# Block products issued across the borders of their groups, with the sums chained in one PSUM bank

## The chip, the cores and the metric

One core of one Trainium2 chip runs the kernel. The metric is the device time of one execution, in microseconds, of which the median over runs is compared. The engines are named as in the profile: PE (TensorE matmuls), PEld (its weight loads), DVE (VectorE), ACT (ScalarE), POOL (GpSimd) and SP, whose queue issues the DMAs.

## What is computed

A decoder layer on 1024 tokens of width 1024 in float32. Three mixers (gated linear attention, mLSTM, forgetting attention) read one wide input projection; their outputs go through one projection each, are merged by sigmoid gates and projected out; a gated MLP with a causal convolution over time follows.

```python
h = rmsnorm(x, norm_mix)
proj = h @ w_in                                   # 1024 x 12312
y = [gla(...), mlstm(...), fox(...)]              # on pieces of proj
branch = jnp.einsum('btnw,nwd->btnd', jnp.stack(y, 2), w_branch)
x = x + jnp.sum(branch * sigmoid(gates + b_gate), 2) @ w_out
h = rmsnorm(x, norm_ffn)
u = causal_dwconv(h @ w_up, conv_w, conv_b)       # 1024 x 5632, three taps
a, g = jnp.split(u, 2, axis=-1)
x = x + (silu(g) * a) @ w_down                    # 2816 rows of w_down
return rmsnorm(x, norm_final)
```

## The kernel before

The four large products (w_in, w_branch, w_up, w_down) are done by a Strassen scheme with seven block products in place of eight. A **job** takes two 128-column units of weights, cut into four blocks a11, a12, a21, a22, and a right side that has been cut and combined into seven operands, `xc[1]` to `xc[7]`. Every float32 operand is split into a high and a low part (`split`, lines 105 to 107: a CAST on ACT, a subtraction on DVE), and a block product (`prod`, line 1081) is twelve matmuls of 128x128 by 128x512: high by high, high by low, low by high, for each of four k-tiles (nine for the first part of w_down, with three k-tiles).

`strassen` (line 1091) issues a job: the products 1 (a11), 5 (sum1), 2 (a12), 6 (sum2), 7 (sum3), 3 (sum4), 4 (a22), in this order. The four weight sums are made on POOL (`comb`, line 1105). Four PSUM banks named `pg` serve a job: a11 and a12 add up in the bank `ba`, sum1 and sum4 in `bc`, sum3 and a22 in `bd`, sum2 has `bb`. Between the two products of a bank its content has to be copied out, since it is a term of other outputs too:

```python
self.prod(ba, self.wsplit(a11, "a11"), xc[1], True)
s1 = keep(ba, "s1")                      # ACT copy, line 1110
...
self.prod(ba, self.wsplit(a12, "a12"), xc[2], False)
...
nc.vector.tensor_tensor(out=s1, in0=s1, in1=bb, op=ALU.add)          # line 1130
...
nc.gpsimd.tensor_tensor(out=s7, in0=s5, in1=s7, op=ALU.add)          # line 1144
```

The four results go to `post`, which adds two terms on DVE and stores (`to_dram`), keeps (`to_tiles`), multiplies by a gate (`merge_pair`, line 1035) or adds to the rows of the result (`down_pair`, line 1262; there POOL takes the terms that lie in SBUF, except in the last part).

The stages follow each other: 48 jobs of w_in, between which the three mixers are issued step by step; three branches of four jobs with w_branch, **the merge**; the output projection; 22 jobs of w_up with convolution and gate (`ffn_up`, line 1232); and w_down in three parts of 6, 8 and 8 k-tiles, four jobs each. Each merge branch and each part of w_down has a right side of its own. `combos` (line 994) makes its seven operands from DRAM: per operand four loads into tiles `yb`, up to four subtractions (tiles `T`, `yb`), four CASTs on ACT and four subtractions on DVE, whose outputs the profile names `x`. The operands lie in 28 fixed slots (`MAP_IN`, `MAP_FF`, `MAP_DN`, lines 36 to 38), so that a new one can be written only when the last job of the group before has used the old one. A list of due times (`due`, with LAG and LAGD) sets when a step of `combos` is issued. I call the stretch where the right side changes **a border**; there are six: gate jobs to branch 1, branch 1 to 2, 2 to 3, up to part 1 of down, part 1 to 2, 2 to 3.

Each engine works through its own queue in order. What stands in the queues is set by a scheduler that orders the instructions of the code by its own estimate of times.

## Time and profile before

| | |
|---|---|
| device time, median of 3 runs | 2527.85 us (2523.35 to 2533.06) |
| the profiled execution: span from first to last instruction | 2538.0 us; no other time of that execution is listed |
| PE busy | 2363.6 us, 93% of the span |
| DVE busy | 1954.1 us, 77% |
| ACT busy | 1255.0 us, 49% |
| POOL busy | 1110.9 us, 44% |
| mean granted TensorE clock | 0.970 of full speed |

The span of the profiled execution is already longer than the median of the runs, by 10.15 us or 0.4%. In the profile a line of `kernel.py` is mostly that of a helper (L99 is every matmul, L107 every low part), so that groups are told apart by the names of their tiles. Matmuls overlap: the duration of one (about 0.4 us) is longer than the distance from one to the next.

### The profile page before, as it was taken

The numbers are of one execution on the slowest core, as the hardware profiler recorded it, in microseconds if no ns is written. First come the engines' busy times: TensorE is split into PE (matmuls) and PEld (weight loads), VectorE is DVE, ScalarE is ACT, GpSimd is POOL, SyncE is SP. The second block draws the span as 40 slices with busy tenths as digits, with TensorE's granted clock in tenths as the row PEclk, the third lists the DMA queues.
The fourth block names the chain that finished last, engine by engine and source line by source line (L and its number), as shares of the span: only waits on it lengthen the run. The fifth ranks groups of instructions, "written<-read, shape, count | busy, mean of one in ns | idle before, by whom it ended". The sixth has DMA issues, their size and how long they took to land. (4 is left out here: it accounts for less than half of the span.)

```text
span 2538.0 us, 34484 instructions
## 1 busy us (share of the span) xinstructions
PE 2363.6 (93%) x11531; PEld 1948.1 (77%) x11531; DVE 1954.1 (77%) x3244; ACT 1255.0 (49%) x2521; POOL 1110.9 (44%) x1018
## 2 busy tenths in 40 slices
PE   6999999899999999999999889799889999978888
PEld 5888788777888888888878768689677777766666
DVE  7886577667777867777777989875888888887896
ACT  5344455455666645555555443344444444453353
POOL 5322265444545543323322347530554444457563
PEclk9999999999999999999999999899899999989899
DMA  3455354554444443433333654444132222235432
GB/s 127 139 165 183 98 171 156 161 160 146 157 138 143 135 149 127 130 122 121 127 127 125 216 172 151 138 138 162 63 116 84 83 75 75 75 115 191 125 112 92
DMA packets 186034, 335.60 MB, mean 132 GB/s; under 512 B 17352, under 2 KB 79336, under 8 KB 185344
## 3 DMA queue, kind: packets, MB, share of 16 engines
q1 hardware_dynamic: 185856, 333.40, 40.4%
q8 instruction: 91, 1.49, 0.2%
q14 instruction: 87, 0.71, 0.1%
HBM read 237.75 MB, written 95.58 MB: 131 GB/s over the span
## 5 line engine op out<-in xcount | busy, mean ns | idle before, releaser
L99 PE MATMUL pg<-x,a12h 128*128 128x512 f32 x744 | 248.3, 416 | 49.1 <-ACT s L1110 47.6
L99 PE MATMUL pg<-x,a22h 128*128 128x512 f32 x744 | 244.0, 408 | 19.2 <-ACT s L1110 13.7
L99 PE MATMUL pg<-x,sum2h 128*128 128x512 f32 x744 | 239.0, 400 | 15.8 <-DVE x L107 12.0
L99 PE MATMUL pg<-x,a11h 128*128 128x512 f32 x744 | 234.6, 396 | 4.8 <-DVE s L1130 2.9
L99 PE MATMUL pg<-x,sum1h 128*128 128x512 f32 x744 | 236.0, 397 | 2.7 <-ACT sum1h L106 2.0
L99 PE MATMUL pg<-x,sum3h 128*128 128x512 f32 x744 | 237.9, 400 | 0.6 <-DVE x L107 0.6
L99 PE MATMUL pg<-x,sum4h 128*128 128x512 f32 x744 | 233.6, 394 | 0.0
L99 PEld LDWEIGHTS pg<-x,a12h 128*128 128x128 f32 x744 | 143.0, 199 | 88.9 <-ACT s L1110 59.1
L99 PEld LDWEIGHTS pg<-x,a22h 128*128 128x128 f32 x744 | 142.9, 196 | 55.8 <-ACT s L1110 17.8
L99 PEld LDWEIGHTS pg<-x,sum2h 128*128 128x128 f32 x744 | 140.1, 191 | 51.3 <-DVE x L107 16.8
L1144 POOL TENSOR_TENSOR s<-s,s 128x512 f32<-128x512 f32 x94 | 132.2, 1406 | 100.5 <-ACT s L1110 87.6
L1110 ACT COPY s<-pg 128x512 f32<-128x512 f32 x280 | 162.1, 579 | 13.8 <-PE pg L99 13.7
L99 PEld LDWEIGHTS pg<-x,a11h 128*128 128x128 f32 x744 | 139.7, 190 | 35.4 <-issue 4.0
L99 PEld LDWEIGHTS pg<-x,sum1h 128*128 128x128 f32 x744 | 139.9, 191 | 31.6 <-ACT sum1h L106 2.4
L99 PEld LDWEIGHTS pg<-x,sum3h 128*128 128x128 f32 x744 | 140.2, 192 | 30.1 <-DVE x L107 1.3
L99 PEld LDWEIGHTS pg<-x,sum4h 128*128 128x128 f32 x744 | 139.9, 190 | 29.9 <-DVE x L107 0.8
L99 PE MATMUL pg<-x,a22l 128*128 128x512 f32 x372 | 151.8, 408 | 10.6 <-DVE a22l L107 10.6
L99 PE MATMUL pg<-x,sum3l 128*128 128x512 f32 x372 | 148.6, 399 | 6.7 <-DVE sum3l L107 6.7
L99 PE MATMUL pg<-x,sum4l 128*128 128x512 f32 x372 | 146.6, 394 | 6.3 <-DVE sum4l L107 6.3
L99 PE MATMUL pg<-x,a12l 128*128 128x512 f32 x372 | 151.5, 407 | 0.0
L99 PE MATMUL pg<-x,a11l 128*128 128x512 f32 x372 | 146.6, 394 | 1.0 <-DVE a11l L107 1.0
L99 PE MATMUL pg<-x,sum2l 128*128 128x512 f32 x372 | 146.7, 394 | 0.0
(472 smaller groups left out, 6585.2 us busy)
## 6 DMA issues: line engine op xcount, KB each, us to landing
up_raw<-in_w_up SPq DMA_DIRECT2D x46, 512.0 KB, 3.6
yb<-y_d SPq DMA_DIRECT2D x84, 256.0 KB, 3.0
yb<-in_w_dn SPq DMA_DIRECT2D x77, 256.0 KB, 3.1
gate_raw<-in_w_in SPq DMA_DIRECT2D x24, 512.0 KB, 3.7
g_d<-st SPq DMA_DIRECT2D x48, 256.0 KB, 2.4
br_raw<-in_w_br SPq DMA_DIRECT2D x24, 512.0 KB, 3.7
gth<-g_d SPq DMA_DIRECT2D x48, 256.0 KB, 2.6
f_d<-c SPq DMA_DIRECT2D x22, 512.0 KB, 2.6
```

Source lines behind the costliest of these rows:

```text
L99: self.nc.tensor.matmul(out, lhsT=lhsT, rhs=rhs, start=start, stop=stop, skip_group_check=skip)
L1110: nc.scalar.copy(out=t, in_=bank)
L1144: nc.gpsimd.tensor_tensor(out=s7, in0=s5, in1=s7, op=ALU.add)
```

## The change

All jobs of the first part (w_in and merge) become one list, all jobs of w_up and w_down another. A generator `products` gives the order of the block products over the whole list: the products 3 and 4 of a job are issued behind the first ones of the next. `gemms` issues the weight split of a product two products ahead of its matmuls. The sums are chained in one bank, `x`: products 1, 6, 7 and 4 of a job add up there, and the bank is read after each of the four; 5 and 3 share the bank `z`, 2 has `y` alone. So s1 + bb and s5 + s7 are no longer added by DVE and POOL. In the merge, up and down, `z` and `y` lie in the other four banks (`pa`). In down every partial sum is added to the result on DVE straight from PSUM, and nothing is copied. The steps of `combos` hang on the products of the last job of the group before. The convolution of a job of w_up is issued in steps between the products of the next ones.

```diff
-MAP_IN = {1: 0, 5: 4, 2: 8, 6: 12, 7: 16, 3: 20, 4: 24}
+MAP_IN = {1: 0, 5: 4, 6: 8, 2: 12, 7: 16, 3: 20, 4: 24}
...
+def products(jobs, lead=0):
...
+        yield j, 1
+        yield j, 5
+        if prev is not None:
+            yield prev, 3
+        yield j, 6
+        if prev is not None:
+            yield prev, 4
+        yield j, 2
+        yield j, 7
+        prev = j
+    yield prev, 3
+    yield prev, 4
...
-            t = pool.tile([P, 512], F32, tag="yb", name="yb", bufs=5)
+            t = pool.tile([P, 512], F32, tag="yb", name="yb", bufs=4)
...
-        hi = self.swp.tile([P, 512], F32R, tag="sh", name=f"{nm}h", bufs=5)
-        lo = self.swp.tile([P, 512], F32R, tag="sl", name=f"{nm}l", bufs=5)
+        hi = self.swp.tile([P, 512], F32R, tag="sh", name=f"{nm}h", bufs=4)
+        lo = self.swp.tile([P, 512], F32R, tag="sl", name=f"{nm}l", bufs=4)
...
+    def compute(self, job, p):
...
+        b = {1: "x", 6: "x", 7: "x", 4: "x", 5: "z", 3: "z", 2: "y"}[p]
+        b = getattr(job, b)
+        self.prod(b, job.w.pop(p), x, p in (1, 5, 2))
+        if acc is not None:
+            if p == 1 or p == 2:
+                acc(0, 0, b)
+            elif p == 6 or p == 3:
+                acc(0, 1, b)
+            elif p == 7:
+                acc(1, 1, job.z)
+                acc(1, 1, b)
+            elif p == 4:
+                acc(1, 0, b)
+        elif p == 1:
+            job.s1 = keep(b, "s1")
+        elif p == 5:
+            job.s5 = keep(b, "s5")
+        elif p == 6:
+            job.u2 = keep(b, "u2")
+        elif p == 2:
+            post(0, 0, job.s1, b)
+        elif p == 3:
+            post(0, 1, job.u2, b)
+        elif p == 7:
+            post(1, 1, job.s5, b)
+        elif p == 4:
+            post(1, 0, b, None)
...
+        for f in job.after.get(p, ()):
+            f()
...
+            while len(due) <= AHEAD:
+                nxt = next(seq, None)
...
+                self.prep(job, p)
+                due.append(nxt)
+            if not due:
+                return
+            self.compute(*due.pop(0))
+            yield
...
+        def add(m, hf, b):
             o = acc[2 * p + m][:, 512 * hf:512 * hf + 512]
...
+            nc.vector.tensor_tensor(out=o, in0=o, in1=b, op=ALU.add)
...
+AHEAD = 2
+ORDER = (1, 5, 6, 2, 7, 3, 4)
...
+            for last, n, b in last_in:
+                hook(last, Lazy(lambda b=b, n=n: merge_combos(b, xcs[n])))
```

The first place: PE in the steady part of w_up, one job before and the same stretch of seven products now. Each row shown is the first of the eight of a product; the number behind `pg` or `pa` tells the banks apart, and a11, sum1 and so on are the weights, which the changed kernel names by product, w1 to w7.

```order
L99 MATMUL pg_20731<-x1_0_18602,a11h_20732 128x512 x2
...
L99 MATMUL pg_20750<-x5_0_19271,sum1h_20753 128x512 x2
...
L99 MATMUL pg_20731<-x2_0_18614,a12h_20771 128x512 x2
...
L99 MATMUL pg_20788<-x6_0_19312,sum2h_20791 128x512 x2
...
L99 MATMUL pg_20808<-x7_0_19361,sum3h_20811 128x512 x2
...
L99 MATMUL pg_20750<-x3_0_19348,sum4h_20832 128x512 x2
...
L99 MATMUL pg_20808<-x4_0_19377,a22h_20849 128x512 x2
```

```order
L143 MATMUL pg_20760<-x1_0_18402,w1h_20711 128x512 x2
...
L143 MATMUL pa_20783<-x5_0_19089,w5h_20735 128x512 x2
...
L143 MATMUL pa_20631<-x3_0_19182,w3h_20756 128x512 x2
...
L143 MATMUL pg_20760<-x6_0_19130,w6h_20779 128x512 x2
...
L143 MATMUL pg_20608<-x4_0_19195,w4h_20799 128x512 x2
...
L143 MATMUL pa_20867<-x2_0_18414,w2h_20817 128x512 x2
...
L143 MATMUL pg_20760<-x7_0_19167,w7h_20839 128x512 x2
```

Before, sum1 alone stands between the two products of the first bank, and sum4 alone between those of the bank of sum3 and a22. Now a bank such as pg_20760 is written by w1, w6 and w7 with two products between each, which belong to the same job or the job before.

The second place: DVE at the border of the second and third merge branch. Rows `x6_..`, `x7_..` and the subtractions into `T` and `yb` make the new right side; `sum2l`, `sum3l`, `w3l`, `w6l` and `w4l` are low parts of weights, one for each block product; `mt` and `gth` belong to the results.

```order
L107 TENSOR_TENSOR x6_2_17285<-T_17197,x6_2_17285 128x512
L1018 TENSOR_TENSOR T_17204<-yb_17288,T_17204 128x512
L107 TENSOR_TENSOR sum2l_17298<-sum2_17295,sum2h_17297 128x512
L1023 TENSOR_TENSOR yb_17314<-T_17183,yb_17314 128x512
L1048 SCALAR_TENSOR_TENSOR gth_17132<-gth_17132,mt_17134 128x512
L107 TENSOR_TENSOR x6_3_17291<-T_17204,x6_3_17291 128x512
L107 TENSOR_TENSOR x7_0_17317<-yb_17314,x7_0_17317 128x512
L1023 TENSOR_TENSOR yb_17320<-T_17190,yb_17320 128x512
L1023 TENSOR_TENSOR yb_17326<-T_17197,yb_17326 128x512
L1023 TENSOR_TENSOR yb_17332<-T_17204,yb_17332 128x512
L107 TENSOR_TENSOR sum3l_17342<-sum3_17339,sum3h_17341 128x512
```

```order
L1051 TENSOR_TENSOR yb_17018<-T_16837,yb_17018 128x512
L151 TENSOR_TENSOR x7_0_17015<-yb_17012,x7_0_17015 128x512
L1051 TENSOR_TENSOR yb_17024<-T_16843,yb_17024 128x512
L151 TENSOR_TENSOR x7_1_17021<-yb_17018,x7_1_17021 128x512
L1051 TENSOR_TENSOR yb_17030<-T_16849,yb_17030 128x512
L151 TENSOR_TENSOR x7_2_17027<-yb_17024,x7_2_17027 128x512
L151 TENSOR_TENSOR w3l_17039<-sum4_17036,w3h_17038 128x512
L151 TENSOR_TENSOR x7_3_17033<-yb_17030,x7_3_17033 128x512
L151 TENSOR_TENSOR w6l_17060<-sum2_17057,w6h_17059 128x512
L151 TENSOR_TENSOR w4l_17079<-br_raw_16720,w4h_17078 128x512
L151 TENSOR_TENSOR x3_0_17102<-yb_17100,x3_0_17102 128x512
```

From the first `x1` row to the last `x4` row of that border DVE's queue holds 63 rows before, 9 of them low parts of weights, and 61 now, 11 of them low parts of weights. Border 1 to 2 has the same counts, the first border 61 and 9 before, 61 and 11 now. From part 1 to 2 of down there are 56 and 10 before, 61 and 11 now; from 2 to 3, 55 and 9 before, 62 and 11 now; into part 1, 45 and 11 before, 43 and 10 now.

The third place: POOL in the first part of down, before and now.

```order
L1144 TENSOR_TENSOR s7_23089<-s5_23040,s7_23089 128x512
L1272 TENSOR_TENSOR acc3_22766<-acc3_22766,s7_23089 128x512
L1273 TENSOR_TENSOR acc3_22766<-acc3_22766,s1_23022 128x512
L1273 TENSOR_TENSOR acc2_22764<-acc2_22764,s1_23022 128x512
L1273 TENSOR_TENSOR acc3_22766<-acc3_22766,s1_23022 128x512
L1105 TENSOR_TENSOR sum1_23147<-dn_raw_23128 128x384
L1105 TENSOR_TENSOR sum2_23179<-sum1_23147,dn_raw_23126 128x384
L1105 TENSOR_TENSOR sum3_23196<-dn_raw_23126,dn_raw_23128 128x384
L1105 TENSOR_TENSOR sum4_23214<-dn_raw_23126,sum2_23179 128x384
```

```order
L1127 TENSOR_TENSOR sum2_22719<-sum1_22665,dn_raw_22641 128x384
L1127 TENSOR_TENSOR sum3_22763<-dn_raw_22641,dn_raw_22643 128x384
L1127 TENSOR_TENSOR sum1_22798<-dn_raw_22781 128x384
L1127 TENSOR_TENSOR sum4_22815<-dn_raw_22641,sum2_22719 128x384
L1127 TENSOR_TENSOR sum2_22832<-sum1_22798,dn_raw_22779 128x384
L1127 TENSOR_TENSOR sum3_22876<-dn_raw_22779,dn_raw_22781 128x384
L1127 TENSOR_TENSOR sum1_22911<-dn_raw_22894 128x384
L1127 TENSOR_TENSOR sum4_22928<-dn_raw_22779,sum2_22832 128x384
L1127 TENSOR_TENSOR sum2_22965<-sum1_22911,dn_raw_22892 128x384
```

POOL keeps the weight sums and loses its adds to the result and the sum s7. Over the whole program POOL has 126 instructions fewer (94 of L1144 and 32 adds to the result), DVE 64 fewer: 94 of L1130 go, and down has 84 adds where it had 64, with a few rows to and fro in the other results. ACT has 44 fewer, SP 2 DMAs fewer (1085). PE has the same 11243 matmuls and transposes.

## Rows read from the trace of the kernel before

**Rows 1.** The page: span, busy times, PE's and the clock's 40 slices.
```profile
span 2538.0 us, 34484 instructions
...
PE 2363.6 (93%) x11531; PEld 1948.1 (77%) x11531; DVE 1954.1 (77%) x3244; ACT 1255.0 (49%) x2521; POOL 1110.9 (44%) x1018
...
PE   6999999899999999999999889799889999978888
...
PEclk9999999999999999999999999899899999989899
```

**Rows 2.** Windows by stretch: length, busy PE, PEld, DVE, ACT, POOL, clock, DMA.
```profile
1542.20:1585.80 43.60, 43.60 (x194) 36.08 (x193) 41.42 (x45) 18.25 (x33) 31.06 (x19) 1.00 0.44 141
...
1396.30:1450.80 54.50, 47.66 (x193) 38.05 (x192) 50.14 (x69) 27.43 (x49) 21.83 (x12) 0.94 0.67 220
1494.40:1542.20 47.80, 39.30 (x145) 30.50 (x144) 43.95 (x54) 17.47 (x31) 28.90 (x16) 0.86 0.55 176
1585.80:1637.80 52.00, 38.80 (x145) 29.85 (x144) 46.22 (x58) 20.12 (x36) 27.43 (x17) 0.87 0.44 145
2212.20:2294.20 82.00, 64.81 (x251) 49.82 (x250) 71.58 (x77) 39.33 (x66) 42.93 (x27) 0.90 0.39 135
2333.90:2391.20 57.30, 42.93 (x151) 32.72 (x151) 55.06 (x64) 21.30 (x38) 31.59 (x19) 0.82 0.48 147
2437.40:2475.20 37.80, 29.37 (x110) 22.93 (x110) 37.36 (x47) 18.01 (x34) 22.86 (x12) 0.86 0.34 108
1797.90:1890.80 92.90, 76.50 (x291) 57.83 (x290) 84.11 (x82) 41.59 (x66) 49.67 (x30) 0.87 0.26 85
1909.90:2212.20 302.30, 289.94 (x1262) 235.45 (x1261) 253.78 (x255) 139.12 (x210) 130.47 (x75) 1.00 0.24 78
0.00:63.00 63.00, 43.00 (x207) 33.78 (x208) 50.31 (x74) 34.48 (x60) 33.88 (x32) 0.92 0.35 128
```

**Rows 3.** The page's groups of PE: busy, mean ns, idle before and its releaser.
```profile
L99 PE MATMUL pg<-x,a12h 128*128 128x512 f32 x744 | 248.3, 416 | 49.1 <-ACT s L1110 47.6
L99 PE MATMUL pg<-x,a22h 128*128 128x512 f32 x744 | 244.0, 408 | 19.2 <-ACT s L1110 13.7
...
L99 PE MATMUL pg<-x,sum4h 128*128 128x512 f32 x744 | 233.6, 394 | 0.0
```

**Rows 4.** Waits of the whole span: total, times, longest.
```profile
DVE ug L1162 <- POOL s L1144: 48.4, 20, 4.6
...
PE pg L99 <- ACT s L1110: 61.3, 35, 8.3
```

**Rows 5.** Waits of PE in the steady part of w_up, 1950 to 2212 us.
```profile
PE pg L99 <- ACT s L1110: 11.6, 12, 1.3
```

**Rows 6.** ACT in order of time at the border of branches 2 and 3.
```profile
1589.40 0.61 ACT L106 CAST sum3h<-sum 128x512 fp32r<-128x512 f32 x1
1595.31 0.62 ACT L106 CAST x<-T 128x512 fp32r<-128x512 f32 x1 [5.29 <-DVE T L1018]
1595.83 0.61 ACT L106 CAST sum4h<-sum 128x512 fp32r<-128x512 f32 x1
1596.35 0.58 ACT L1110 COPY s<-pg 128x512 f32<-128x512 f32 x1
```

**Rows 7.** Groups by form: what is removed, and what takes its place.
```profile
L1110 ACT COPY s<-pg 128x512 f32<-128x512 f32 x280 | 162.1, 579 | 13.8 <-PE pg L99 13.7
...
L1130 DVE TENSOR_TENSOR s<-s,pg 128x512 f32<-128x512 f32 x94 | 64.0, 681 | 34.7 <-PE pg L99 34.3
L1144 POOL TENSOR_TENSOR s<-s,s 128x512 f32<-128x512 f32 x94 | 132.2, 1406 | 100.5 <-ACT s L1110 87.6
...
L1272 DVE TENSOR_TENSOR acc<-acc,pg 128x512 f32<-128x512 f32 x24 | 16.3, 679 | 8.0 <-PE pg L99 8.0
L1273 POOL TENSOR_TENSOR acc<-acc,s 128x512 f32<-128x512 f32 x24 | 37.6, 1583 | 4.7 <-PE pg L99 2.3 <-DVE acc L1272 1.8
...
L107 DVE TENSOR_TENSOR x<-yb,x 128x512 fp32r<-128x512 f32 x115 | 107.3, 966 | 0.3 <-ACT x L106 0.3
```

More of the change, by code (lines that the diff above doesn't have):

```diff
@@ L1099, in strassen, with prep @@
             raw.append(r)
-        a11, a12, a21, a22 = (raw[i][:, H * k:H * k + H] for i in range(2) for k in range(2))
-        lead = s1 is not None
+        job.raw = [raw[i][:, H * k:H * k + H] for i in range(2) for k in range(2)]
+    def prep(self, job, p):
+        a11, a12, a21, a22 = job.raw
+        H = P * job.nk
         def comb(a, b, op, nm):
-            t = wp.tile([P, 512], F32, tag="ws", name=nm, bufs=3)[:, 0:H]
-            nc.gpsimd.tensor_tensor(out=t, in0=a, in1=b, op=op)
-            return t
@@ new lines, in comb @@
+            self.nc.gpsimd.tensor_tensor(out=t, in0=a, in1=b, op=op)
+            return t
+        if p == 1:
+            src = a11
+        elif p == 2:
+            src = a12
+        elif p == 4:
+            src = a22
+        elif p == 5:
+            src = job.sum1 = comb(a21, a22, ALU.add, "sum1")
+        elif p == 6:
+            src = job.sum2 = comb(job.sum1, a11, ALU.subtract, "sum2")
+        elif p == 7:
+            src = comb(a11, a21, ALU.subtract, "sum3")
+        else:
+            src = comb(a12, job.sum2, ALU.subtract, "sum4")
@@ new lines, in gemms @@
+    def gemms(self, jobs, lead=0):
+        seq = products(jobs, lead)
+        due = []
+        while True:
+            while len(due) <= AHEAD:
+                nxt = next(seq, None)
+                if nxt is None:
+                    break
+                job, p = nxt
+                if job.raw is None:
+                    self.load_w(job)
+                self.prep(job, p)
[3 more added lines that the diff above has]
+            self.compute(*due.pop(0))
+            yield
@@ L1300, in pool, with hook @@
         return tc.tile_pool(name=name, bufs=1, side=side, reuse_waits="tile", **kw)
+    def hook(job, gen):
+        for p in ORDER:
+            job.after.setdefault(p, []).append(lambda: next(gen))
     with ExitStack() as ctx:
@@ L1335, in body @@
             mix = mixers()
-            for n, _ in enumerate(stream):
+            for n in range(12, 12 + 7 * 45):
+                next(stream)
                 next(mix, None)
@@ new lines, in body, with down_combos @@
+        tiles = Tiles()
+        chunks, k0 = [], 0
+        for nk in DN_CHUNKS:
+            chunks.append((k0, nk))
+            k0 += nk
+        xcs = [{} for _ in chunks]
+        acc, dn = [], {}
+        def down_combos(c, dst):
+            k0, nk = chunks[c]
+            return k.combos(dn["pool"], nk // 2,
+                            lambda kh, i, hf: a["w_dn"][k0 + kh * (nk // 2) + i][:, 512 * hf:512 * hf + 512],
+                            dst, MAP_FF, k.nc.vector if c else k.nc.gpsimd)
@@ new lines, in ffn @@
+        def ffn():
+            jobs = list(k.ffn_jobs(xc, tiles, bg))
+            last = jobs[-1]
+            for c, (k0, nk) in enumerate(chunks):
+                hook(last, Lazy(lambda c=c: down_combos(c, xcs[c])))
+                for p in range(4):
+                    jobs.append(k.down_job(p, k0, nk, acc, xcs[c]))
+                    if c == len(chunks) - 1:
+                        jobs[-1].done = lambda p=p: dn["done"].extend((2 * p, 2 * p + 1))
+                last = jobs[-1]
+            return jobs
@@ L1377, in body @@
+        stream = k.gemms(ffn(), LEADS)
         with pool("oh") as hp:
@@ new lines, in body @@
+        counts = [0]
+        with pool("ffn") as fp:
+            tiles.pool = fp
+            while counts[0] < NFF:
+                if counts[0] == LEADS and "pool" not in dn:
+                    right.close()
+                    dn["pool"] = right.enter_context(pool("dn", side="right"))
+                    for i in range(2):
+                        acc.append(dn["pool"].tile([P, D], F32, name=f"acc{i}"))
+                        k.nc.sync.dma_start(out=acc[i], in_=k.x2_d[i])
+                next(stream)
+                for _ in range(4 if counts[0] + len(bg) == NFF else 1):
+                    background()
```

378 lines of the change are left out of this document (175 added, 203 removed).

## The prediction, made before the changed kernel ran

> **What bounds the kernel now.** I read the page first [rows 1]. PE is busy 93% of the span; the next engine, DVE, 77%. In PE's 40 slices the low digits stand between 55 and 75% of the span and in the last eighth, and the clock's digits fall in about the same slices. So PE is the bound for long stretches, and something else for a few.
>
> The windows say which stretches [rows 2]. The first row, 1542.20 to 1585.80, holds sixteen block products without a stall: 43.6 / 16 = 2.725 us a product, 0.2271 us a matmul. I call that the full pace. A window's count of matmuls, less the one to three that straddle its edges, times 0.2271 us is the time it would need at that pace; the rest is lost. For the six borders in order of time: 192 matmuls, 43.6 of 54.5 us, 10.9 lost; 144, 32.7 of 47.8, 15.1 lost; 144, 32.7 of 52.0, 19.3 lost; 249, 56.5 of 82.0, 25.5 lost; 150, 34.1 of 57.3, 23.2 lost; 108, 24.5 of 37.8, 13.3 lost. Sum: 107.3 us. The start of w_up (288 matmuls, 65.4 of 92.9) loses 27.5, the steady part of w_up (1260, 286.1 of 302.3) loses 16.2.
>
> In the same rows DVE is busy 50.1 of 54.5, 44.0 of 47.8, 46.2 of 52.0, 71.6 of 82.0, 55.1 of 57.3 and 37.4 of 37.8 us: at the borders DVE has the least room, while the clock is down to 0.82 to 0.94. In the steady part of w_up DVE has 254 of 302 us and the clock is 1.00: there the loss is a wait, not a full engine.
>
> Which wait, the groups of PE show [rows 3]: of the idle time before a12, 47.6 us ended with the copy `s` on ACT, before a22 13.7 us. Both are the second product of a bank that must be copied first, with one product between. The third such product, sum4, has three products between and no idle time. Over the span these waits are 61.3 us in 35 cases, the longest 8.3 [rows 4]; in the steady part of w_up 11.6 us in 12 cases, at most 1.3 each [rows 5]. Why a copy of 0.58 us is late by more than a product shows on ACT at the border of branches 2 and 3 [rows 6]: ACT stood idle 5.29 us for a subtraction `T` on DVE, then did the cast, another cast, and the copy. The copy was ready to go and stood behind a cast that waited for DVE.
>
> **The change part by part.** *More distance in a bank.* Product 6 now follows 1, and 7 follows 6, with two products between; 4 follows 7 with four, 3 follows 5 with seven. A copy may be 5.4 us late instead of 2.7. In the steady part of w_up no wait exceeded 1.3 us [rows 5], so all 11.6 us go, and I take 13 of the 16.2 lost, since the DVE adds that waited 48.4 us for the sum on POOL [rows 4] no longer do. After that PE should run w_up at full pace; DVE, at 254 of 302 us, is next. In the mixers the same waits are few; I take 4 us.
>
> *Borders, merge.* Between the first and last row of the new right side DVE has 61 or 63 rows before, with 9 low parts of weights, and 61 with 11 now. Each low part feeds one product. While DVE works off the border, PE gets two products more: 2 x 2.725 = 5.4 us less loss for each border. The two rows that go from the second and third are worth 1.4 us at 681 ns [rows 7]. DVE's rows are also drawn out by POOL: the rows `x` from `yb` take 966 ns on average, against 681 for a row of the same size that reads a bank [rows 7]. POOL loses 94 sums of 1.41 us; I take 2 us a border for that and for the waits on POOL. Together 7.4, 8.8 and 8.8: 25 us of 45.3.
>
> *Borders, down.* POOL's 32 adds of about 1.58 us [rows 7] go, DVE gains 20 adds of 679 ns. From part 1 to 2 the border has 5 rows more and one low part more: 5 x 0.68 = 3.4 us against one product, 2.7. From 2 to 3 7 rows more, 4.8 us, against two products, 5.4. That alone gives nothing. The gain is that the waits on ACT's copy have no copy any more, and that POOL, busy 31.6 of 57.3 us in that window [rows 2], keeps the four sums of a job out of some eight rows; I take 8 and 6 us, an estimate between nothing and the 23.2 and 13.3 lost. Into part 1 the border has 2 rows fewer, and the convolution comes in steps, not all at once: I take 12 of 25.5. Sum 26 us of 62.0.
>
> *Starts.* At the beginning and at the start of w_up two jobs instead of one give PE products 1 and 2 while operands 5, 6 and so on are made. DVE is busy 50.3 of 63 and 84.1 of 92.9 us there [rows 2] and makes as many operands as before, so PE only moves later work forward. Four more products before the first window ends would be 11 us; I take 6 for each start, 12 together.
>
> *At nothing.* The evacuation of w_up, of w_in and of the merge has the same number of ACT copies or one less; PE hides them. Weight splits have four buffers instead of five: 5.4 us ahead instead of 8.2, hidden as long as ACT and DVE have room, and a stall of PE by a late low part if not. Weights are loaded when product 1 is prepared, three products or 8.2 us ahead, and SP's queue also passes the loads of the right side, issued seven products earlier than before: four tiles `yb` instead of five, with `T` loaded directly. If SP waits for a `yb`, the weights behind it come late, and POOL's sum1, ACT's cast and PE follow. I bound that between nothing, since the loads are as many, and 3 us a border, the stall of POOL turned into PE time; I take nothing. The mixers are interleaved anew; bounds of 10 us to either side, taken as zero because PE's slices there are already at 90% or more [rows 1].
>
> Sum: 13 + 4 + 25 + 26 + 12 = 80 us. Against the profiled span that is 2538.0 - 80 = 2458.0 us; the median of the runs lies 10.15 us below that span, so 2527.85 - 80 = **2448 us**, 3.2% faster.
>
> A second account gives the lower bound. If only the waits for the copy are touched, the gain lies between the 11.6 us of w_up [rows 5] and the whole 61.3 us [rows 4]; halfway, 36 us, is 2491. The upper bound is all border loss: 107.3 + 16.2 + 12 + 4 = 140 us.
>
> Against the change speaks a rule of the Trainium skill ("PSUM — Partial Sum Buffer", Summary: rules for kernel authors): a bank is read while matmuls run on another one, not on the same. By it the chain is the wrong shape, because three of its four products wait for a reader; the rows show that such a wait costs nothing at a distance of three products [rows 3]. By the rule the time would be the first rival's 2581 us, by those rows 2448.
>
> **The rivals.** *The chain serialises* (slower). The bank `x` is read once more per job, and in down all its readers are DVE adds that stand behind the new right side in DVE's queue. If two products of distance don't cover the reader, each of 92 jobs pays at least the read itself, 0.579 us [rows 7]: 53 us, with nothing gained: 2581 us. It decides from the point where readers are over 5.4 us late. For it: ACT's copy was once 8.3 + 2.7 us late [rows 4]. Against it: one of 35 cases. This is the case that the rule of the Trainium skill (the same page and section) would mean.
>
> *DVE stays the bound at the borders.* DVE has no room there [rows 2] and as many rows as before; PE would then wait for low parts instead of copies. Left are 13 + 4 and about 10 from the borders: 2501 us.
>
> *The borders are covered.* The work of a border may now spread over seventeen products (46 us) instead of thirteen, because products 3 and 4 of the last job come later. If DVE finds the room, the upper bound: 2388 us.
>
> *The change doesn't do what it says.* The queues show that it does; but the new waits could give back what the old ones cost: 2528 us, within 0.5%.
>
> **How the numbers follow.** Forecast 0.57 (2410 to 2490), DVE stays the bound 0.20 (2490 to 2515), borders covered 0.10 (2385 to 2410), no net change 0.07, serialised 0.06. The range 2400 to 2510 holds the forecast, most of the second and part of the third case, about 0.8. What a measurement can tell from no change is 0.5%, 12.6 us. Faster by more: 0.57 + 0.10 + most of 0.20, 0.85; within it 0.08; slower by more 0.07.
>
> **What would show it.** Right: in the profile of the changed kernel a job in the steady part of w_up takes 84 x 0.2271 = 19.1 us instead of 302.3 / 15 = 20.15, no wait of PE for an `s` copy there; the border windows lose 6 to 13 us each, still with DVE nearly full and PE waiting for low parts `w..l` or `x`; POOL's busy time falls by some 180 us (94 x 1.41 + 32 x 1.58). Wrong: PE waits for `acc` or `u2` in many places (the chain serialises), the mixers' stretch grows by more than 10 us, or the borders lose as much as before.

## The result, and the profile after

The changed kernel takes 2464.86 us, median of four runs (2460.64 to 2467.23), against 2528.36 us for the kernel before (median of four, one run more than the table ahead of the prediction has); the ratio is 0.9748 with an interval of 0.9732 to 0.9764. That is 63.5 us or 2.5% less, against 80 us predicted; on a second chip the ratio was 0.9748 again.

The page of the changed kernel, the lines that answer to [rows 1]:

```profile
span 2458.5 us, 34199 instructions
...
PE 2333.9 (95%) x11531; PEld 1933.2 (79%) x11531; DVE 1856.2 (75%) x3180; ACT 1246.0 (51%) x2477; POOL 903.8 (37%) x892
...
PE   7999999989999999999999999899989999988898
...
PEclk9999999999999999999999999899989999999999
```

The work of PE is the same, 11531 matmuls and transposes in both profiles. POOL has 207 us less, DVE 98 us less. The clock's digits show fewer dips, and the long run of nines covers the mixers and w_up; of its two eights one lies at the third merge border, the other at the start of w_up.

PE's busy time falls too, from 2363.6 us [rows 1] to 2333.9, for the same work. So of the 79.5 us between the two spans 49.8 are idle time of PE that went, and 29.7 are matmuls that ran faster: the trace has the clock at one of two levels, 1.2 or 2.4 GHz, and PE was at the lower one for some 150 us before and some 84 now (mean granted clock 0.970 and 0.983). So the clock gave something on top of the waits; the second pair of profiles below has 18 us for it.

The windows, the counterparts of [rows 2] (length, busy PE, PEld, DVE, ACT, POOL, clock, DMA): the merge borders 1 to 3, the three borders of down, the start of w_up, its steady part, the beginning.

```profile
1382.80:1431.60 48.80, 42.23 (x181) 33.49 (x182) 43.69 (x61) 27.07 (x47) 14.29 (x11) 1.00 0.71 238
1472.40:1520.00 47.60, 42.54 (x181) 33.22 (x180) 41.65 (x57) 18.86 (x35) 19.70 (x14) 1.00 0.63 208
1550.00:1599.00 49.00, 37.92 (x132) 28.61 (x131) 45.31 (x59) 20.12 (x36) 30.11 (x16) 0.83 0.49 165
2157.00:2237.00 80.00, 68.13 (x271) 53.72 (x270) 78.11 (x83) 40.61 (x66) 34.92 (x21) 0.91 0.40 129
2274.50:2340.50 66.00, 59.79 (x247) 47.81 (x246) 52.51 (x76) 21.34 (x36) 19.83 (x14) 0.95 0.44 136
2359.60:2424.60 65.00, 60.00 (x253) 47.87 (x252) 50.46 (x75) 24.25 (x41) 18.60 (x16) 0.97 0.36 117
1760.30:1850.20 89.90, 80.46 (x346) 63.72 (x345) 81.85 (x85) 46.52 (x76) 48.77 (x29) 0.92 0.27 95
1850.20:2154.90 304.70, 304.70 (x1346) 252.29 (x1345) 274.86 (x258) 155.69 (x225) 128.16 (x65) 1.00 0.25 83
0.00:63.00 63.00, 45.35 (x224) 38.24 (x225) 47.03 (x73) 33.55 (x58) 32.88 (x31) 0.92 0.33 124
```

In the steady part of w_up PE is busy without a gap: 304.70 / 1346 = 0.2264 us a matmul, a job of 84 in 19.0 us. The third merge border alone looks as before: PE 37.92 of 49 us, the clock at 0.83, POOL busy 30.11 us.

What PE still waits for (engine, line, releaser: total, times, longest), to be held against [rows 4]:

```profile
PE pg L143 <- DVE w1l L151: 17.5, 7, 4.4
...
PE pa L143 <- DVE w3l L151: 12.1, 6, 4.6
PE pg L143 <- DVE x L151: 11.1, 7, 2.4
...
PE pa L143 <- DVE w5l L151: 5.4, 3, 4.6
...
PE pg L143 <- ACT u L1155: 2.5, 3, 1.8
...
PE pg L143 <- DVE mt L1074: 2.2, 1, 2.2
...
PE pg L143 <- DVE acc L1334: 1.4, 1, 1.4
```

The 61.3 us for the copy `s` are gone. What is left at the borders are low parts on DVE, of weights (`w1l` and so on) and of operands (`x`). The last three lines are all the waits for a reader of the chained bank: five, 6.1 us. (The rows left out that are longer than 3 us belong to the mixers, to `w7l` or to a load.)

**The loss by stage.** To hold two kernels side by side, each stage's length less the time of its matmuls at the undisturbed pace (0.2271 us for 512 columns; for other shapes the lower quartile of their spacing in the changed kernel), summed over the trace. Stages are cut where a job's first product starts. The two kernels have the same matmuls, so a difference of losses is a difference of time. The loss holds both kinds, the idle time of PE and the matmuls at the lower clock. Gains in us, of the pair shown so far and of a second pair of profiles (e1 below against e5 below):

| stage | predicted | first pair | second pair |
|---|---|---|---|
| beginning | 6 | 4.3 | 6.4 |
| mixers | 4 | 7.0 | 2.0 |
| merge border 1 | 7.4 | 2.5 | 0.9 |
| merge border 2 | 8.8 | 8.4 | 6.7 |
| merge border 3 | 8.8 | -0.1 | 3.4 |
| end of the merge, output projection | 0 | -2.0 | -6.7 |
| start of w_up | 6 | 15.1 | 13.8 |
| steady part of w_up | 13 | 17.8 | 18.1 |
| into part 1 of down | 12 | 7.3 | 6.0 |
| part 1 to 2 | 8 | 12.1 | 10.8 |
| part 2 to 3 | 6 | 5.8 | 4.5 |
| after that | 0 | 1.3 | 1.3 |
| sum | 80 | 79.5 | 67.0 |

The sums are the differences of the spans, 2538.0 - 2458.5 and 2532.1 - 2465.1 (the rounded rows of the second column add up to 0.2 more). The first is above the 63.5 us of the medians: the first profile of the kernel before was a long execution, and that of the changed kernel was the fastest of its four, 4.2 us below their median. A stage is uncertain by 2 to 5 us, as the columns show, the mixers by as much again: e6 and e10 below lose 4 us more there than e5, though their edits don't touch the mixers. The stage "steady part" has 17 jobs, the window of [rows 2] from which the prediction took 16.2 us lost has 15.

### The profile page after: what moved, and what is told of

Read it like the earlier page. It is cut to its first block, busy times and chain, and to the rows that moved or that the text cites. A ratio compares the mean times of both kernels' runs of the same rounds, so it can differ in the third digit from the quotient of the medians.

```text
span 2458.5 us, 34199 instructions
## 1 busy us (share of the span) xinstructions
PE 2333.9 (95%) x11531; PEld 1933.2 (79%) x11531; DVE 1856.2 (75%) x3180; ACT 1246.0 (51%) x2477; POOL 903.8 (37%) x892
## 5 line engine op out<-in xcount | busy, mean ns | idle before, releaser
L143 PE MATMUL pg<-x,w6h 128*128 128x512 f32 x744 | 239.0, 400 | 12.7 <-DVE x L151 11.1
L143 PE MATMUL pg<-x,w7h 128*128 128x512 f32 x744 | 235.4, 397 | 2.6 <-ACT u L1155 2.5
L143 PE MATMUL pg<-x,w1h 128*128 128x512 f32 x744 | 236.0, 397 | 0.1
L143 PE MATMUL pg<-x,w4h 128*128 128x512 f32 x744 | 231.9, 392 | 3.1 <-DVE mt L1074 2.2
L143 PEld LDWEIGHTS pg<-x,w6h 128*128 128x128 f32 x744 | 140.4, 192 | 46.6 <-DVE x L151 15.3
L143 PE MATMUL pg<-x,w1l 128*128 128x512 f32 x372 | 148.7, 400 | 17.5 <-DVE w1l L151 17.5
L143 PEld LDWEIGHTS pg<-x,w1h 128*128 128x128 f32 x744 | 140.0, 191 | 28.8 <-DVE x L151 0.5
L143 PE MATMUL pg<-x,w7l 128*128 128x512 f32 x372 | 147.2, 396 | 3.8 <-DVE w7l L151 3.8
L143 PE MATMUL pg<-x,w6l 128*128 128x512 f32 x372 | 147.1, 395 | 0.0
L143 PE MATMUL pg<-x,w4l 128*128 128x512 f32 x372 | 145.2, 390 | 1.0 <-DVE w4l L151 1.0
```

What stands on the lines that cost most here:

```text
L143: self.nc.tensor.matmul(out, lhsT=lhsT, rhs=rhs, start=start, stop=stop, skip_group_check=skip)
```

## The experiments

Ratios below are to the kernel before on the same chip; the changed kernel has 0.9748. Half the width of an interval is some 0.0015, 4 us, so a difference of two ratios is known to about 5 us.

**e1, the kernel before again.** No edit.

> The kernel before, unchanged, profiled a second time. Its first profile has a span of 2538.0 us, 10 us above its median; the changed kernel's span of 2458.5 us lies 6 us below its own median, so the two spans differ by 79.5 us and the medians by 63.5. Theory: the first profile was a long execution, and the stages where the second one is shorter are not gains of the change: span 2520 to 2532. Rival: the kernel before is longer by some 10 us whenever it is profiled: 2535 to 2541. What differs by stage between the two profiles bounds how finely a gain can be put down to a stage; I expect up to 5 us in a stage.

```profile
span 2532.1 us, 34484 instructions
...
PE 2353.1 (93%) x11531; PEld 1937.2 (77%) x11531; DVE 1955.3 (77%) x3244; ACT 1253.7 (50%) x2521; POOL 1103.2 (44%) x1018
```

2532.1 us, 0.1 us above the theory's range and well below the rival's. Its whole time, 2533.93 us, is 2 us below the median of the runs on its chip (2536.31), where the first profile's span is 10 us above its own. So the first was a long execution, and that excess is no gain of the change. It was long in PE's busy time (2363.6 us against 2353.1, at a mean clock of 0.970 against 0.975), not in its waits: PE is idle 174.4 us there and 179.0 here. With e5 below (PE 2335.3 us of 2465.1) this second pair gives 49 us of idle time and 18 us of faster matmuls: the gain in waits agrees in the two pairs, the gain by the clock does not (30 and 18). Its stages differ from the first profile's by up to 4 us either way; the second column of the table rests on it.

**e2, no product crosses into the next job.**

```diff
         yield j, 1
         yield j, 5
-        if prev is not None:
-            yield prev, 3
         yield j, 6
-        if prev is not None:
-            yield prev, 4
         yield j, 2
         yield j, 7
...
+        yield j, 3
+        yield j, 4
```

(and the same for the jobs that are started ahead).

> The changed kernel with one thing undone: no product crosses into the next job; each job is 1, 5, 6, 2, 7, 3, 4. The chain in one bank, the banks, the copies and the direct adds stay. Three products of a job then wait for a reader of the bank with one product between (1 to 6, 6 to 7, 7 to 4). Theory (distance decides): in the steady part of w_up the waits for a copy or an add are back, a job takes 20 to 20.5 us in place of 19.07, some 15 us over that stage, and each of six borders loses the two products, 6 x 5.4 = 32 us: 2510 us, range 2490 to 2530. Rival (the chain itself and the adds taken off POOL and DVE make the gain): w_up stays at 19.1 us a job, the borders within 10 us: 2465 to 2475.

0.9779 (0.9763 to 0.9795): 8 us slower, near the rival. The steady part of w_up and the waits of PE:

```profile
1875.00:2170.00 295.00, 295.00 (x1304) 244.27 (x1303) 246.12 (x250) 149.39 (x215) 108.45 (x63) 1.00 0.26 84
```

```profile
PE pg L139 <- DVE acc L1330: 19.0, 4, 7.9
...
PE pa L139 <- DVE acc L1330: 9.9, 2, 5.3
PE pg L139 <- DVE mt L1070: 8.9, 3, 3.6
...
PE pg L139 <- ACT u L1151: 7.0, 4, 2.4
PE pg L139 <- ACT s L1151: 6.4, 4, 3.4
```

Full pace, with one product between two writes of the chained bank. So distance did not cure the steady part. Elsewhere it does count: of the readers of that bank PE waits 19.0 us in four cases for an `acc` add, which stands on DVE behind the new right side, and with `mt`, `u`, `s` and two short rows some 45 us in 19 cases, against 6.1 us in five cases in the changed kernel. (The two waits at `pa` are for bank z: three products stand between its writes, but its first reader is issued only behind product 7, right before product 3.) The loss at the borders of down is 10 us more than in e5 (5.4 at 1 to 2, 4.6 at 2 to 3), at merge border 2 it is 5.7 more; other stages give some back, and the time is 8 us longer.

**e3, one job started ahead, not two.**

```diff
-            stream = k.gemms(watched(), LEADS)
+            stream = k.gemms(watched(), 1)
...
-        stream = k.gemms(ffn(), LEADS)
+        stream = k.gemms(ffn(), 1)
```

(and the counts of products issued during the two starts follow).

> The changed kernel with one job instead of two started ahead, at the beginning and at the start of w_up; nothing else. I had put 6 us on each start; the profiles show about 18 and 15. Theory (the second lead is worth what I predicted, the rest of the two gains comes from the new order of products 7 and 3 and the convolution in steps): +12 us, 2472 to 2482. Rival 1 (the second lead is all of it): +33 us, 2490 to 2500. Rival 2 (PE only moves work, and waits later for the same operands): within 5 us of 2465.

0.976 (0.9745 to 0.9775): within 3 us of the changed kernel, not separable, rival 2. By losses the beginning is 5.6 us worse than in e5, the start of w_up 0.5 us. The second lead is worth its 6 us at the beginning and nothing at w_up, where the gain of 14 has another cause. The 18 us in the expectation was my misreading: I compared when a job began, but the work issued up to there differs. Up to the start of the fifth job, where the first stage of the table ends, the changed kernel has issued 504 matmuls and transposes, the one before 605; 24 of the 101 missing are the two products held back, the other 77 come later as well. The table above counts work and says 4 to 6.

**e4, the merge's subtractions on POOL.**

```diff
-                            MAP_IN, k.nc.vector)
+                            MAP_IN, k.nc.gpsimd)
```

> The changed kernel with the subtractions T and yb of the three merge borders on POOL in place of DVE, 16 for a border. Theory (DVE's queue still limits these borders, PE waits there for low parts): 16 x 0.68 to 1.0 = 11 to 16 us of DVE work go from each border, whose losses are some 7, 6 and 19 us; the time falls by 8 to 16 us, 2449 to 2457, and the waits of PE for w1l, w5l and w7l at these places go. Rival (the operands' own chain of load, subtraction, cast, subtraction limits them): POOL takes 1.4 to 2.0 us for each in place of 0.7 to 1.0, 16 x 0.8 = 13 us longer at each border, and the weight sums stand behind them: slower by 5 to 25 us, 2470 to 2490.

0.9837 (0.9822 to 0.9852): 23 us slower; the rival, its sign and size. Two of the four groups of subtractions, now POOL's:

```profile
L1043 POOL TENSOR_TENSOR T<-yb,T 128x512 f32<-128x512 f32 x12 | 21.0, 1778 | 12.5 <-DMA yb<-y_d 12.5
L1059 POOL TENSOR_TENSOR yb<-yb,T 128x512 f32<-128x512 f32 x12 | 19.8, 1662 | 2.1 <-DVE w1l L151 2.1
```

In the merge the means of the four groups are 1.56 to 1.78 us. The three borders lose 7.5, 9.4 and 8.3 us more than in e5, and PE's wait for w3l in the merge grows from 4.3 to 11.8 us: what DVE was relieved of, the chain of the operands and the weight sums behind them paid. It also shows that DVE's amount of work is not what sets these borders: each lost 16 of its rows and became longer.

**e5, the changed kernel again**, as control for the next three. No edit.

> The changed kernel, unchanged, as the one the other three of this group are held against on the same chip. Both theories: the ratio to the kernel before is 0.975 again, within 0.0016.

0.9748 (0.9733 to 0.9762).

```profile
PE 2335.3 (95%) x11531; PEld 1932.7 (78%) x11531; DVE 1860.9 (75%) x3180; ACT 1249.0 (51%) x2477; POOL 901.7 (37%) x892
```

**e6, the convolution of a job at once.**

```diff
-                if next(g, bg) is bg:
-                    bg.remove(g)
-                    counts[0] += 1
+                for _ in g:
+                    pass
+                bg.remove(g)
+                counts[0] += 1
```

> The changed kernel with the convolution and gate of a job of w_up issued all at once when the job's last product is issued, as the kernel before did, in place of in steps between the products of the next jobs. The run without products across jobs kept the full pace in the steady part of w_up at a distance of one product, so the distance isn't what removed the waits there. Theory 1 (the steps did): a job of w_up takes 19.8 to 20.3 us in place of 19.05, PE waits for copies or adds there, and the stage gives back 13 to 18 us: 8 to 18 us above the unchanged one. Rival (the work taken off POOL and DVE did, or the split two products ahead): the same within 4 us, a job at 19.0 to 19.2 us.

0.9739 (0.9724 to 0.9753), the same; w_up at 295.00 us for 1303 matmuls, the full pace. The steps are worth nothing by themselves.

**e7, no splitting ahead.**

```diff
-AHEAD = 2
+AHEAD = 0
```

> The changed kernel with the weights of a product split when its own matmuls are issued, not two products ahead; order of products, chain and banks stay. Theory 1 (splitting ahead puts casts and low parts in front of the readers of the banks, and so takes PE's waits for low parts away): without it PE waits for low parts w1l to w7l in many places, also in the mixers, 15 to 40 us slower. Rival (the scheduler puts them as early anyway, and the readers come first again): within 6 us of the unchanged one.

0.9825 (0.9805 to 0.9844): 20 us slower, theory 1. PE's waits, with e5's 18.4 us for w1l as the measure:

```profile
PE pg L143 <- DVE w1l L151: 25.9, 8, 6.0
...
PE pa L143 <- DVE w2l L151: 9.5, 3, 6.2
...
PE pa L143 <- ACT w5h L150: 6.5, 3, 4.5
```

Against e5 the loss grows by 5 us at the beginning, 7 in the mixers, 7 at merge border 2, 3 into part 1 of down and 5 at part 1 to 2; in w_up not at all. The 5 us at the beginning are slower matmuls, not waits: PE is idle 19.8 us there in e5 and 19.5 here. `AHEAD` is the largest single part that the runs found, and my sum had no term for it. But it sets more than the split: when the weights are loaded and when POOL makes their sums goes with it, and the 4.5 us wait for `w5h` ended with such a sum, for which ACT stood idle. How much is the split, how much the sums and loads, the run doesn't part; where I write splitting ahead below, it is all three. Its profiled execution was the longest of four, 6 us above their median, so its stages add up to 29 us, not 20.

**e8, one POOL add a job put back.**

```diff
+        if p == 7 and acc is None:
+            nc.gpsimd.tensor_tensor(out=job.s1, in0=job.s5, in1=job.s5, op=ALU.add)
```

> The changed kernel with one more POOL addition in each of the 82 jobs of w_in, merge and w_up: it adds the copy s5 to itself into the dead copy s1, 128x512, as the kernel before added s5 and s7; nothing reads the result. Theory (the relief of POOL, and with it of DVE's stretched rows, is a part of the gain): POOL's busy time grows by 82 x 1.4 = 115 us, DVE's low parts of sums take some 10% longer, and the time grows by 6 to 15 us. Rival (POOL has room and nothing waits for it): within 4 us.

0.9799 (0.9782 to 0.9815): 13 us slower, the theory's size. The page:

```profile
PE 2343.9 (94%) x11531; PEld 1937.0 (78%) x11531; DVE 1896.9 (76%) x3180; ACT 1246.6 (50%) x2477; POOL 1010.8 (41%) x974
```

and the added group, and the row of DVE that grew most (72.1 us in e5):

```profile
L1192 POOL TENSOR_TENSOR s<-s 128x512 f32<-128x512 f32 x82 | 114.5, 1397 | 89.4 <-DVE st L1236 55.4 <-DVE mt L1074 11.4 <-ACT s L1155 8.7
```

```profile
L1305 DVE SCALAR_TENSOR_TENSOR c<-u,cols,c 128x1023 f32<-128x1023 f32 x42 | 85.0, 2024 | 0.0
```

114.5 us of work that nothing reads cost 36 us of DVE's time (1896.9 against e5's 1860.9) and 13 us in all. The details of the theory hold in part: the low parts did not grow (961 of them, 803 us in e5, 799 here), the convolution's rows did, where DVE has room. Against e5 the loss grows in the mixers (7 us, where e6 and e10 show 4 without a cause), the merge borders (5), the beginning (3, by slower matmuls, not by waits) and the projection (2). The added row also waits for DVE in POOL's queue (89.4 us idle before it), with the weight sums behind it: ACT's wait for a sum before w5h is 53.3 us instead of 39.8. How much is that wait and how much DVE's stretched rows, the run doesn't tell.

**e9, e2 and e6 together.** Edits as there.

> Both edits that each left the steady part of w_up at the full pace, together: no product crosses into the next job, and the convolution and gate of a job are issued all at once at its end. In the kernel before, at 1932 us, the copy s of product a11 stood on ACT behind a convolution step that waited for DVE, and PE waited 1.3 us. Theory (the convolution's steps at the head of ACT's queue make the reader late, and a distance of one product doesn't cover that; either the steps or the crossing cures it): a job of w_up takes 19.6 to 20.3 us in place of 19.04, PE waits there for ACT's s or u, and the time is 8 to 20 us above the run without crossing alone, 2488 to 2500 us against a kernel before of 2536. Rival (the DVE add and the POOL add that are gone did it, which both edits keep away): 19.0 to 19.2 us a job, the time within 4 us of the run without crossing alone, a ratio of 0.977 to 0.979.

0.9795 (0.9779 to 0.9812): with e2's within the interval. The steady part:

```profile
1869.00:2165.00 296.00, 296.00 (x1308) 245.09 (x1307) 247.38 (x250) 151.48 (x217) 109.59 (x63) 1.00 0.26 84
```

Full pace; the rival. Neither the crossing nor the steps are needed there.

**e10, down through copies.**

```diff
-        def add(m, hf, b):
+        def post(m, hf, x, y):
             o = acc[2 * p + m][:, 512 * hf:512 * hf + 512]
-            nc.vector.tensor_tensor(out=o, in0=o, in1=b, op=ALU.add)
+            if y is None:
+                nc.vector.tensor_tensor(out=o, in0=o, in1=x, op=ALU.add)
+            else:
+                eng = nc.vector if k0 + nk == NFF else nc.gpsimd
+                nc.vector.tensor_tensor(out=o, in0=o, in1=y, op=ALU.add)
+                eng.tensor_tensor(out=o, in0=o, in1=x, op=ALU.add)
...
-        return Job(src[0], src[1], xc, None, "dn", nk=nk // 2, wide=True, acc=add)
+        return Job(src[0], src[1], xc, post, "dn", nk=nk // 2, wide=True)
```

> The changed kernel with the down product through copies, as in the other stages: products 1, 5 and 6 of a job are copied by ACT, and the two terms of an output are added one after the other, the copied one on POOL except in the last part (3 POOL adds and 4 DVE adds a job in place of 7 DVE adds). Order, chain and splitting ahead stay. Theory (the direct adds are worth what I put on the borders of parts 1 to 2 and 2 to 3, 8 and 6 us, since POOL is kept out of DVE's rows and no copy is waited for): 8 to 16 us slower than the unchanged one, ratio 0.978 to 0.981. Rival (DVE is the limit at these borders, and three rows of 0.68 us a job fewer on it pay for the copies): within 4 us or faster, ratio 0.972 to 0.976.

0.9755 (0.9741 to 0.977): the rival. At part 1 to 2 the loss is 5.7 us more than in e5, and 2.2 less into part 1; the sum is 2 us, not separable. The edit brings back both the copies that PE may wait for and POOL's adds, so the 5.7 us are for the two together. POOL's adds take 1.7 us each:

```profile
L1339 POOL TENSOR_TENSOR acc<-acc,s 128x512 f32<-128x512 f32 x16 | 27.4, 1717 | 17.4 <-DVE acc L1338 17.4
```

**e11, splitting three products ahead.** `AHEAD = 3`.

> The changed kernel with weights split three products ahead in place of two, in the same four buffers. Without any splitting ahead it was 20 us slower. Theory (PE's waits for low parts at the borders, some 40 us with w1l, w3l, w5l and w7l, are a matter of their place in DVE's queue, and one product more puts them in front of the rows of the right side): these waits halve and the time falls by 5 to 15 us, ratio 0.969 to 0.973. Rival (DVE has no room at the borders: what a low part gains in its place an operand x loses): within 4 us, ratio 0.973 to 0.976; or the buffers are taken too early and nothing moves.

0.9756 (0.9728 to 0.9783): the rival. PE's waits for w1l leave the head of the list, and others take their place:

```profile
PE pg L143 <- DVE acc L1334: 12.7, 7, 4.3
...
PE pa L143 <- ACT w3h L150: 9.0, 3, 5.4
```

The rival gave two reasons, no room on DVE or buffers taken too early; the run doesn't tell which.

**e12, the old readers put back in w_up**, on top of e9.

```diff
+        elif p == 7 and job.name == "up":
+            s7 = keep(b, "s7")
+            nc.gpsimd.tensor_tensor(out=s7, in0=job.s5, in1=s7, op=ALU.add)
+            post(1, 1, s7, None)
...
-                nc.scalar.copy(out=dst, in_=x)
+                if up:
+                    nc.vector.tensor_copy(out=dst, in_=x)
+                else:
+                    nc.scalar.copy(out=dst, in_=x)
```

> The run without crossing and with the convolution at once kept w_up at 19.04 us a job, so neither the order of products nor the steps removed the waits of the kernel before. Left are the two outputs whose last reader the chain has changed: output (1,1) was added by POOL and then by DVE, output (1,0) was added by DVE and is now copied by ACT itself, from the bank. This run puts both back for w_up alone, on top of the run without crossing and with the convolution at once: s7 is copied, POOL adds s5, DVE moves it to its place; the last output is moved by DVE. ACT's queue then has the copy s of product 1 behind two convolution steps, of which the second waits for DVE's move, which stands behind a convolution row of 1.3 to 2.0 us on DVE, as in the kernel before. Theory (the chain's own readers made the difference): a job of w_up takes 19.8 to 20.3 us in place of 19.04, PE waits there for s, and the time is 13 to 22 us above the run it is built on: ratio 0.985 to 0.988. Rival (the load of DVE and POOL over the stage, not the place of these rows): 19.0 to 19.2 us a job, ratio 0.979 to 0.981.

0.9832 (0.9815 to 0.9848): 9 us above e9, but only 4 of them in the steady part, where a job takes 295.00 / 1288 x 84 = 19.24 us; another 7 lie before and behind it in w_up, and some in the merge, which the edit doesn't touch. Between theory and rival. The trace lists no wait of PE in the window below, but 30 of its matmuls, two a job, come some 0.1 us later than at the full pace, 3.0 us together. All 30 are in product 6, the one that PE may start only when the copy `s` of product 1 is out of the bank; in e9 none is late. One old reader was not put back, the add of `bb` to `s1` on DVE.

```profile
1880.00:2175.00 295.00, 295.00 (x1288) 240.25 (x1287) 256.02 (x261) 144.29 (x213) 140.35 (x78) 1.00 0.26 84
```

ACT in order of time, here and in e1 at the same place of a job (start, us, line, operation, what ended the idle time before):

```profile
2006.35 1.25 ACT L1302 ACTIVATE c<-u,cols 128x1024 f32<-128x1024 f32 x1 [1.96 <-DVE u L1221]
2007.50 0.60 ACT L146 CAST w7h<-sum 128x512 fp32r<-128x512 f32 x1
2008.01 0.57 ACT L1151 COPY s<-pg 128x512 f32<-128x512 f32 x1
```

```profile
1928.50 1.24 ACT L1249 ACTIVATE c<-ug,cols 128x1024 f32<-128x1024 f32 x1 [2.29 <-DVE ug L1162]
1929.65 0.60 ACT L106 CAST sum4h<-sum 128x512 fp32r<-128x512 f32 x1
1930.15 0.57 ACT L1110 COPY s<-pg 128x512 f32<-128x512 f32 x1
```

The same queue in both: the convolution's second half waits for a result that DVE moves late, a cast follows, then the copy that PE needs. In e12 it ends at 2008.58 and PE's product starts at 2008.6, just in time; in e1 it ends at 1930.72, 1.3 us late. So the chain, by which the last output is copied by ACT itself and the other needs no POOL, takes this queue apart; that it is the whole cause isn't shown. In e1 DVE also stood 2.44 us for POOL's `s` before it came to `ug`, 5 us earlier and for the other half of `ug`, so that the link to this wait of ACT is likely, not shown:

```profile
1923.08 0.69 DVE L1162 TENSOR_TENSOR ug<-s,s 128x512 f32<-128x512 f32 x1 [2.44 <-POOL s L1144]
```

Old readers without splitting ahead, which may be what brings the 1.3 us back, were not tried, nor was the old order of operands in w_up (7 before 3).

## Why the prediction was right, and where it was not

The forecast (2448 us, range 2400 to 2510, faster) held with 2464.86. Of its ground two parts held: PE is the bound, and the waits for copies are what can go. That DVE limits the borders was not shown. At the last two borders of down DVE is busy 52.51 of 66 and 50.46 of 65 us in the windows above, and e4 took 16 rows a border off it and lost time. Of the signs that it named, the job of 19.1 us and the missing waits for `s` came true; the border windows lose some 8, 7, 19, 19, 10 and 8 us, two of them above the 6 to 13 named; POOL fell by 207 us, not 180. Step by step:

- *Steady part of w_up, 13*: measured 18 over 17 jobs, which over the 15 jobs of the prediction's window is all of the 16.2 us lost; a job takes 19.0 us, as foretold. The step that failed is its reason, "a copy may be 5.4 us late instead of 2.7": e2 and e9 have one product between and keep the full pace. By e12, where only the product behind the copy `s` is late, the queue in front of the copy is at least a part of the cause.
- *Mixers, 4, and beginning, 6*: measured 2 to 7 and 4 to 6. For the beginning e3 shows the lead as cause.
- *Start of w_up, 6*: mis-sized, measured 14 to 15. The reason, the second lead, is not it (e3: 0.5 us). In e1 PE waits there 7.6 us for copies `s`, which the changed kernel doesn't:

```profile
PE pg L99 <- ACT s L1110: 7.6, 3, 4.8
```

  Of the first pair's 15.1 us 9.2 are idle time of PE and 5.9 matmuls that ran faster, at a mean clock of 0.92 in the stage after 0.89. e2 and e12 give back about 3 us each. The rest isn't settled; two further changes here, a fourth buffer for raw weights (three before) and the order of operands 7 and 3, were never taken back.
- *Merge borders, 25*: mis-sized, measured 11. "PE gets two products more: 5.4 us less loss for each border" holds for the second border alone. Why it fails at the other two is open. POOL's time beside DVE goes with the gain at two of them: in the window of border 2 it went from 28.90 of 47.80 us [rows 2] to 19.70 of 47.60, at border 3 it stayed at 30.11 of 49.00 against 27.43 of 52.00 [rows 2], since the jobs of the second branch add into `mg` on POOL. But at border 1 it fell too, from 21.83 of 54.50 us [rows 2] to 14.29 of 48.80, for a gain of 1 to 2.5 us. At border 3 the `mg` adds also hold SP's queue. The waits of SP's queue there:

```profile
SPq L1071 <- POOL mg L1079: 10.7, 3, 7.3
```

and the queue itself, and ACT:

```profile
1549.15 2.73 SPq L1027 DMA_DIRECT2D yb<-y_d  x2
1559.21 0.32 SPq L1071 DMA_DIRECT2D gth<-g_d  x1
1559.63 0.86 SPq L1027 DMA_DIRECT2D yb<-y_d  x2
```

```profile
1563.13 0.62 ACT L150 CAST x<-yb 128x512 fp32r<-128x512 f32 x1 [3.95 <-DMA yb<-y_d]
```

  A gate's load waits 7.3 us for one of two buffers that POOL gives back, the next operand's loads stand behind it, ACT waits 3.95 us for them, and DVE, and PE 4.6 us for w5l. The prediction had SP's queue as a danger the other way round, weights behind operands, at nothing to 3 us. This is loss that remains, not loss that the change brought: around border 3 SP's queue waited 43.4 us in 12 cases for `mg` before and 38.5 us in 12 now. A third buffer for the gates was not tried.
- *Borders of down, 26*: measured 25 and 21, each within 6 us of its own term. Of the reason for 1 to 2 and 2 to 3, POOL kept out and no copy to wait for, e10 shows 5.7 us at the first and nothing at the second, and paid for elsewhere. The distance in the bank (e2) and splitting ahead (e7) show 5 us each at 1 to 2.
- *At nothing*: the end of the merge lost 2 to 7 us that were not foreseen. Splitting ahead, only thought of as a danger to the buffers, is worth 20 us over the kernel (e7), and three products ahead nothing more (e11). POOL's relief, put at 2 us a merge border, cost 13 us in all when an add was put back (e8). These parts overlap with the terms of the sum and can't be added to them. The faster matmuls, 18 to 30 us of the gain, are no term either: they are inside the losses that it counted, without being told from the waits.

That the total came near is in part luck, because two errors nearly cancel: merge and projection 16 to 21 us too high, the two parts of w_up 13 to 14 too low. The 16 us between 80 and 63.5 are as much as the first pair of profiles stands above the medians, some 12 by the long first execution and 4 by the fast one of the changed kernel; by the second pair, 67.0 us, the sum was 13 too high.

*The chain serialises* did not come true. After a chained product PE waits nowhere for long: of 94 jobs (the prediction says 92) five have such a wait, 6.1 us together, for `u`, `mt` and `acc`. The rival's point of decision did show in e2, where with one product of distance these waits are some 45 us and the time is 8 us longer. The rule of the Trainium skill ("PSUM — Partial Sum Buffer", Summary: rules for kernel authors) is to read another bank than the one matmuls run on. Here it is met mostly by time: with two products or more between, the reader is nearly always done before PE writes the bank again, and the waits for these readers are the 6.1 us.

## What to carry to other kernels

A bank that is chained and read between its products cost little here, 6 us of waits with two or more products between, and nothing in the steady part of w_up even with one; look at what stands in front of the reader, before counting products. Where PE waits for split weights, issue their preparation a couple of products ahead: here the cheapest line and the largest part that a run found. Part an engine's gain into idle time and busy time: for the same work PE was faster as well as less idle. And compare two kernels by loss at equal work, not by when a job starts: my first reading was off by a factor of three or more.

## What was not expected of the hardware

How long a row of DVE takes depends on what it reads and on whether POOL works meanwhile. The groups of the changed kernel over the whole span, all 128x512:

```profile
L151 DVE TENSOR_TENSOR x<-yb,x 128x512 fp32r<-128x512 f32 x115 | 91.6, 819 | 5.1 <-ACT x L150 5.1
L151 DVE TENSOR_TENSOR w3l<-sum,w3h 128x512 fp32r<-128x512 f32 x90 | 84.4, 938 | 1.0 <-ACT w3h L150 0.9
...
L1234 DVE TENSOR_TENSOR st<-s,pg 128x512 f32<-128x512 f32 x88 | 60.0, 682 | 52.9 <-PE pg L143 52.7
...
L1334 DVE TENSOR_TENSOR acc<-acc,pg 128x512 f32<-128x512 f32 x48 | 32.4, 680 | 10.6 <-PE pg L143 10.6
```

The groups that read a bank average 680 and 682 ns. Rows with both inputs in SBUF average 819 to 938, with single ones at 1.78 us. Row by row over the same trace, for all of DVE's TENSOR_TENSOR of 128x512:

| | rows | mean, ns | longest, ns |
|---|---|---|---|
| an input in a bank, POOL working or not | 394 | 682 | 693 |
| both inputs in SBUF, no POOL row at the time | 636 | 683 | 696 |
| both inputs in SBUF, beside a POOL row | 357 | 1141 | 1824 |

So a row with both inputs in SBUF is drawn out only beside POOL, and a row that reads a bank is not. With less of POOL's work `x<-yb` fell from 966 [rows 7] to 819, and with 82 adds more on POOL (e8) the convolution's rows grew from 1716 to 2024. The Trainium skill ("SBUF — State Buffer", SBUF: two separate sides) has a lock on a pair of ports, which a DVE row with two SBUF inputs and a POOL row that reads SBUF exclude each other from; the rows above agree with it. That an add moved from POOL into an add from PSUM on DVE is worth more than its own time would follow, but isn't shown: e8 put POOL rows back and also held up POOL's queue, and e10 found nothing separable.
